# The first five levels of a DeltaNet chunk inverse on 32x32 diagonal squares of the TensorE array

## The chip, the cores and the metric

The kernel runs on one core of one Trainium2 chip, as one program. What is measured is device time in microseconds (us) of that core; the profile adds one traced execution with the start and end of every instruction on every engine. Of the engines, PE is the matrix unit (TensorE), PEld its loading of stationary operands (weights), DVE, ACT and POOL the vector, scalar and GpSimd engines, SP the queue that issues most DMAs.

## The reference

Two layers of a backbone. In each, 768 tokens (256 context, 512 latent) are projected, go through differential attention, grouped-query attention and a bidirectional gated DeltaNet side by side, are merged, and go through a channel mixer. The change is in the DeltaNet:

```python
a_low = jnp.where(strict, jnp.einsum('bhncd,bhnsd->bhncs', kb, kc) * decay, 0.0)
tmat = lax.linalg.triangular_solve(a_low + eye, jnp.broadcast_to(eye, a_low.shape),
                                   left_side=True, lower=True, unit_diagonal=True)
u = tmat @ (vc * bc[..., None])
w = tmat @ (kb * jnp.exp(gcum)[..., None])
```

For every chunk of tokens, head and direction, the inverse of a unit triangular matrix I + A is wanted. The kernel uses chunks of 128 tokens, so that a matrix fills a 128x128 square.

## The kernel before

The work on PE is of two kinds. The *lane* is long products: projections of all tokens with weights that are streamed from memory, written as runs of matmuls of 512 or 256 columns (their PSUM tiles are called `pf`, their weights `wl`). *Chains* are short dependent pieces: attention heads, norms, and the DeltaNet; their PSUM tiles are `pm` (one bank) and `pb`. A planner (`Sched`, with the estimate `Est` of when each engine gets through its queue) decides, as the program is built, which piece is queued next: a chain's piece when its inputs are estimated to be ready within 0.1 us, otherwise the next matmul of the lane. Every engine then works off its own queue strictly in that order. All recorded operations have one line, L166, that of the helper that records them, so groups are told apart by their tiles.

`dn_prep` is the chain that the change touches. It is run once for each of six steps of two pairs of heads in two layers, 24 times in all, each time for four units (two directions, two heads) that lie side by side in tiles of 512 columns. `a32` is I + A in float32, `a16` its float16 copy; both lie in workspace slots named `pres`. `u16` and `t16` (the inverse's transpose and the inverse, slots named `dnw`) start as the inverse of the diagonal and are doubled seven times, from blocks of 1 to blocks of 64:

- level 0: four matmuls of 128 columns with the identity transpose `a16` into a bank `py`; DVE masks it with `lev` into `u16`, and masks `a16` into `t16` in two more instructions;
- levels 1 to 6: four matmuls `a16` by `u16` of 128 columns into `py`; DVE multiplies the bank by the level's mask `lev` into `ym` (a `pres` tile); then four matmuls of 128 columns into `pt` and four of 64 columns into `pu`; ACT copies `pt` to `t16`, DVE the new columns from `pu` to `u16`;
- two Newton steps in higher precision follow, and then the scan over the chunks (`dn_pair`).

So each level puts two groups of matmuls on PE, with a DVE piece between them and an ACT and a DVE piece behind them, and in these pauses the planner queues the lane or another chain. Elsewhere in the program, `mod_mm` (the modulation, tiles `wm` and `wr` by `cond`) already divides the array by columns: its matmuls have 32 output rows each, at four places in turn.

Of the kernel before, what the change touches and what calls it, by code (L numbers as in the profile page):

```python
# [14 lines left out]
BF16 = mybir.dt.bfloat16  # L15
# [23 lines left out]
NLEV = 7  # L39
BIG = 1e30  # L40
# [33 lines left out]
class Est:  # L74
    """An estimate of when each engine gets through what is queued to it; it decides only the order in which
    independent pieces of work are queued."""
# [8 lines left out]
    def keys(self, ap):  # L85
        """The banks of a PSUM tile; the parts of a tile that was cut into views."""
# [12 lines left out]
    def cost(self, e, op, out, ins):  # L99
        n = out.free_size()  # L100
        if e == "P":
            cyc = (2 if op == "transpose" else 4) if ins[-1].dtype == F32 else 1
            return (max(n, 64) / 2.4 + 4) * (1 if out.shape[0] == 32 else cyc)
# [32 lines left out]
    def take(self, tag, t):  # L136
        """A tile of PSUM takes the place of the one that was given back first."""
        q = self.idle[tag]
        at = min(q)
        q.remove(at)  # L140
        for i in range(4 * t.tensor.shape[1] // 2048):
            self.done[t.tensor.name, i] = {"": at}, {}
        return t

    def give(self, tag, t):
        """A tile that nothing queued from here on touches."""
# [3 lines left out]
    def free(self, tag, n):  # L150
        """When the next n tiles of the tag can be had."""
        return sorted(self.idle[tag])[n - 1]
# [21 lines left out]
class Sched:  # L174
    """Queues chains of short dependent pieces as they become ready, and in between pieces of long products
    (the lane), of which one at a time is under way.

    A chain is a generator; it yields what its next piece needs: PSUM tags ("m", "mm", "b", ...), a time in ns
    to wait, or a condition (a function of true, or of the time from which it holds). A product is (units, body): units, the weights' sources; body(tiles) a generator."""
# [14 lines left out]
    def defer(self, gen, bank=None):  # L194
        """Work off the tensor engine, to be queued when the engines come to it; gen yields the engine of its next
        instruction, or a condition that an earlier group fulfils. It is the last to read bank."""
# [13 lines left out]
    def at(self, g):  # L210
        """When the next instruction of a group could start."""
# [4 lines left out]
    def settle(self):  # L216
        """Queues of the deferred work what would start soon."""
# [15 lines left out]
    def prefetch(self):  # L233
        """The first job's weights."""
# [3 lines left out]
    def flush_banks(self, n):  # L238
        """Leaves at most n banks of the lane to be read."""
# [4 lines left out]
    def stream(self, items, width, prio=0):  # L244
        """Chains (condition, generator, first need) in order, `width` of them at a time."""
        self.streams.append([list(items), width, prio, []])

    def room(self, need):
        """Whether the tiles are there: "w" slots of the workspace, "V" and "W" with one and with `reserve` to spare,
        "t" temporaries, "r" raw weights; "m", "b" PSUM."""  # L250
# [35 lines left out]
    def pick_fill(self, more):  # L286
        """A job that only fills gaps, of which there are so many and `more` to use."""
# [90 lines left out]
def trunk(  # L378
# [4 lines left out]
    rope, ident_d, tri_d, sel_d, m12_d, lev_d,  # L383
# [21 lines left out]
    def open_pools(nb, nm):  # L405
        """PSUM besides the feature projections' banks: nb pairs of banks and nm banks, until close_pools."""
# [12 lines left out]
    def whole(parts, n, nm, dt=F32):  # L419
        """One 6 KB slot of the workspace, in parts of n columns."""  # L420
# [9 lines left out]
    def q_tiles():  # L430
        """Per query chunk: four transposed columns of 128."""
        return slot(3, 512, "qt", F32R) + slot(3, 512, "qt", F32R)

    def drop(n=1):
        """n slots that nothing queued from here on touches."""
# [18 lines left out]
    def give(*banks):  # L454
        """Banks of psml that nothing queued from here on touches."""
# [22 lines left out]
    lev = const.tile([P, NLEV, 2, P], BF16, name="lev")  # L478
    nc.gpsimd.dma_start(out=lev, in_=lev_d)
    ones = const.tile([P, 1], F32, name="ones")  # L480
# [4 lines left out]
    def rsqrt_small(dst, src):  # L485
        """dst = src ** -0.5 on GpSimd; both [128, n] in SBUF."""
        G.tensor_tensor(out=dst, in0=src, in1=mhalf[:, 0:src.shape[1]], op=ALU.pow)

# [1 line left out]
    lo_n = [0, 3]  # L490

    def wunit(src, n):
        """A unit of weights, hi and lo, and the group that splits it."""
# [20 lines left out]
    def split(hi, lo, src, eng=None):  # L514
        """hi + lo == src, each with what a float32r matmul keeps."""
# [26 lines left out]
    def mod_mm(ps, raw, q, i, first, last):  # L542
        """256 columns of the modulation, of both streams at once, from half q of k: partitions 32 j + 2 i and the next
        sum over k = j and j + 4 (mod 8), the others get zeros; mod_sum adds them up and turns them to feature-major."""
# [4 lines left out]
    def mod_sum(m, b, sb, c0, n):  # L549
        """n pairs of column chunks from c0 on."""  # L550
# [9 lines left out]
    def mod_gen(m, b, cb, raws):  # L560
        """Four column chunks of the modulation."""
# [9 lines left out]
    def mod_late(l, m, b, pairs, room, pace):  # L571
        """A chain: up to MOD_N pairs of column chunks, the raw weights in slots of the workspace or in those of the products'."""
# [53 lines left out]
    def norm_acc(x, nt, out=None, fin=None, sq1=None):  # L626
        """Sums of squares over the chunks of x, as they come: add(chunk, first token, last) is a group; stats(first
        token, last) then gives the rows of (mean(x * x) + eps) ** -0.5 on all partitions of a bank. fin(first token,
        last, condition) is called when the last chunk has come; stats may be called once the condition holds."""
# [1443 lines left out]
```

## Time and profile before

| | |
|---|---|
| time, median of 3 runs | 2926.34 us (2926.0 to 2927.13) |
| span of the profiled execution | 2919.9 us |
| PE busy | 2847.6 us, 98% |
| PEld busy | 2466.7 us, 84% |
| DVE busy | 1693.0 us, 58% |
| ACT busy | 1226.7 us, 42% |
| POOL busy | 801.8 us, 27% |
| mean granted TensorE clock | 0.995 |

The busy time of an engine is the union of its instructions. For PE that is no measure of how fast it goes, since a matmul is listed from its start to the modelled end of its results, while the next one starts earlier; the distance from start to start is what a matmul costs its successors. The DeltaNet's preparations lie in two stretches, from about 575 to 930 us (layer one) and from 2140 to 2430 us (layer two).

### The profile page before, as it was taken

How to read it: one execution, taken by the hardware profiler on the slowest of the kernel's cores; microseconds unless marked ns; L12 is line 12 of the kernel's file. 1: busy time of each engine (PE TensorE's matmuls, PEld its weight loads, DVE VectorE, ACT ScalarE, POOL GpSimd, SP SyncE). 2: the span in 40 equal slices, each digit the busy share in tenths (PEclk: the TensorE clock that was granted, in tenths of full speed). 3: DMA queues.
4: the chain of work that ended last, by engine and by line, in shares of the span. 5: the costliest groups of instructions: out<-in, count | busy, mean ns of one | idle time of the engine just before them, and what ended most of it. 6: DMA issues, size and time to landing. Idle time of an engine off the chain costs nothing. (4 is left out here: it accounts for less than half of the span.)

```text
span 2919.9 us, 48983 instructions
## 1 busy us (share of the span) xinstructions
PE 2847.6 (98%) x19399; PEld 2466.7 (84%) x19399; DVE 1693.0 (58%) x3432; ACT 1226.7 (42%) x2522; POOL 801.8 (27%) x832
## 2 busy tenths in 40 slices
PE   7999999999999999999999999999999999999999
PEld 5888898888888888888888888998888787888888
DVE  4555667867766544334333456567788777553343
ACT  4444656644444223213222345466655443343332
POOL 3314231022322332102121233432133323422221
PEclk9999999999999999999999999999999999999999
DMA  8242211142112632342212222121111125323332
GB/s 300 95 146 82 68 47 56 48 157 66 65 57 84 242 105 93 113 124 68 73 49 75 76 97 66 36 78 55 61 41 45 55 72 185 130 87 104 97 99 87
DMA packets 96596, 268.82 MB, mean 92 GB/s; under 512 B 13808, under 2 KB 22896, under 8 KB 96368
## 3 DMA queue, kind: packets, MB, share of 16 engines
q1 hardware_dynamic: 85280, 244.13, 25.7%
q10 hardware_dynamic: 10800, 20.98, 1.8%
q8 instruction: 153, 2.51, 0.4%
q0 software_dynamic: 288, 0.59, 0.1%
q14 instruction: 75, 0.61, 0.1%
HBM read 237.41 MB, written 28.84 MB: 91 GB/s over the span
## 5 line engine op out<-in xcount | busy, mean ns | idle before, releaser
L166 PE MATMUL pf<-hh,wl 128*128 128x512 f32 (+1 forms) x4192 | 1020.8, 359 | 9.4 <-ACT hh L166 6.1
L166 PEld LDWEIGHTS pf<-hh,wl 128*128 128x128 f32 x4192 | 696.4, 189 | 106.6 <-issue 10.1
L166 POOL TENSOR_TENSOR wl<-wr,wl 128x512 fp32r<-128x512 f32 (+3 forms) x258 | 322.4, 1266 | 970.7 <-ACT wl L166 966.6
L166 PE MATMUL pf<-hl,wl 128*128 128x512 f32 (+1 forms) x2096 | 580.0, 359 | 0.9 <-POOL hl L166 0.5
L166 ACT CAST wl<-wr 128x512 fp32r<-128x512 f32 (+3 forms) x620 | 340.8, 589 | 491.8 <-PE pf L166 366.3
L166 PEld LDWEIGHTS pf<-hl,wl 128*128 128x128 f32 x2096 | 360.4, 189 | 47.5 <-issue 2.5
L166 PE MATMUL pf<-wl,hh 128*128 128x256 f32 (+2 forms) x1664 | 322.2, 288 | 0.0
L166 PE MATMUL pf<-g,wl 128*128 128x512 f32 (+1 forms) x1629 | 309.2, 350 | 0.0
L166 DVE TENSOR_TENSOR wl<-wr,wl 128x512 fp32r<-128x512 f32 (+4 forms) x362 | 260.9, 745 | 76.3 <-ACT wl L166 74.7
L166 PEld LDWEIGHTS pf<-g,wl 128*128 128x128 f32 x1629 | 263.4, 189 | 44.9 <-issue 2.9
L166 PEld LDWEIGHTS pf<-wl,hh 128*128 128x128 f32 x1664 | 265.0, 193 | 6.0 <-issue 4.1
L166 PE MATMUL pf<-wl,hl 128*128 128x256 f32 (+2 forms) x832 | 241.3, 290 | 0.0
L166 DVE SCALAR_TENSOR_TENSOR x<-pf,gate,x 128x512 f32<-128x512 f32 (+1 forms) x126 | 80.3, 639 | 230.5 <-PE pf L166 230.4
L166 PE MATMUL pm<-dnw,pres 128*128 128x128 f16 (+1 forms) x1824 | 197.2, 236 | 6.7 <-DVE dnw L166 2.1
L166 ACT ACTIVATE p<-pb,nb,r 128x768 f32<-128x768 f32 (+1 forms) x160 | 145.1, 908 | 104.8 <-DVE nb L166 82.9
L166 DVE SCALAR_TENSOR_TENSOR ff<-pf,cf,ff 128x511 f32<-128x511 f32 (+1 forms) x132 | 86.8, 658 | 172.9 <-ACT ff L166 171.5
L166 PE MATMUL pf<-ohl,wl 128*128 128x512 f32 (+1 forms) x864 | 168.2, 355 | 0.4 <-DVE th L166 0.4
L166 PEld LDWEIGHTS pf<-wl,hl 128*128 128x128 f32 x832 | 160.3, 193 | 2.7 <-issue 2.5
L166 PEld LDWEIGHTS pf<-ohl,wl 128*128 128x128 f32 x864 | 142.2, 189 | 23.4 <-DVE th L166 0.8
L166 DVE TENSOR_REDUCE mx<-pb 128x1 f32<-128x768 f32 (+1 forms) x160 | 133.5, 845 | 43.0 <-PE pb L166 41.8
L166 POOL TENSOR_TENSOR g<-ff,g 128x768 fp32r<-128x768 f32 (+1 forms) x44 | 69.8, 1586 | 256.8 <-ACT g L166 256.8
L166 ACT CAST dnw<-pm 128x512 f16<-128x512 f32 x144 | 83.8, 585 | 129.9 <-PE pm L166 124.5
(243 smaller groups left out, 4123.1 us busy)
## 6 DMA issues: line engine op xcount, KB each, us to landing
wr<-in_w_dram SPq DMA_DIRECT2D x88, 512.0 KB, 3.5
wr<-in_w_f_dram SPq DMA_DIRECT2D x80, 512.0 KB, 3.6
wm<-in_w_mod_dram SPq DMA_DIRECT2D x72, 512.0 KB, 6.2
wr<-in_w_t_dram SPq DMA_DIRECT2D x32, 512.0 KB, 3.6
wr<-in_w_br_dram SPq DMA_DIRECT2D x24, 512.0 KB, 3.6
wr<-in_w_mod_dram SPq DMA_DIRECT2D x24, 512.0 KB, 3.5
wr<-in_w_dram SPq DMA_DIRECT2D x32, 384.0 KB, 3.1
wr<-in_w_dram SPq DMA_DIRECT2D x32, 320.0 KB, 2.9
```

The costliest lines, as they stand in the source:

```text
L166: ins = f(*args, **kw)
```

## The change

Levels 0 to 4 fill blocks of at most 32, so they act within the four 32x32 squares on the diagonal of each unit. The changed kernel takes these squares out of `a32` (four ACT copies of 32 partitions and 4 x 32 columns, one for each square's partitions, into `ac`), and does levels 0 to 4 on tiles of 128 partitions and 4 x 32 columns, in which the partitions 32q to 32q + 31 hold square q of each unit. A matmul of such a level takes its weights and its moving operand from partitions 32q on and writes to partitions 32q on, so it uses one of four 32x32 places on the diagonal of the array; the helper `squares` issues 16 of them, unit by unit, the four places in turn. Level 0 is one such group of 16; levels 1 to 4 are a group of 16 and one of 32 each. The masks (`sub`) and copies then handle 128 columns instead of 512, and the copy of both results is one ACT instruction of 256 columns. At the end of level 4 two DVE instructions of 512 columns spread the squares over the full tiles `u16` and `t16`, with zeros elsewhere (`own`). Levels 5 and 6 and the Newton steps are as before, with a shorter `lev`. The planner prices a 32x32 matmul of up to 32 columns at 9 ns. Comments and docstrings were removed, which shifts lines: L166 is L170 in the changed kernel.

```diff
@@ class Est: cost
         if e == "P":
+            if out.shape[0] == SUB and n <= SUB:
+                return 9
             cyc = (2 if op == "transpose" else 4) if ins[-1].dtype == F32 else 1
@@ constants
-    lev = const.tile([P, NLEV, 2, P], BF16, name="lev")
+    lev = const.tile([P, NLEV - NSUB, 2, P], BF16, name="lev")
     nc.gpsimd.dma_start(out=lev, in_=lev_d)
+    sub = const.tile([P, NSUB + 1, 2, SUB], BF16, name="sub")
+    nc.gpsimd.dma_start(out=sub, in_=sub_d)
+    own = const.tile([P, P // SUB, SUB], BF16, name="own")
+    nc.gpsimd.dma_start(out=own, in_=own_d)
@@ dn_prep
+        for q in range(0, P, SUB):
+            S.copy(out=ym[q:q + SUB, 0:P].rearrange("p (u c) -> p u c", u=4), in_=a3[q:q + SUB, :, q:q + SUB])
         S.copy(out=a16, in_=a32)
...
+        def squares(out, a, b):
+            for u in range(4):
+                for q in range(0, P, SUB):
+                    r = slice(q, q + SUB)
+                    T.matmul(out[r, u * SUB:(u + 1) * SUB], lhsT=a(r, u), rhs=b(r, u), start=True, stop=True)
...
+        def masked(out, src, m):
+            V.tensor_tensor(out=d4(out), in0=d4(src), in1=sub[:, m].unsqueeze(2).to_broadcast([P, 2, 2, SUB]), op=ALU.mult)
+        ac, yc, tc_, uc_ = [ym[:, i * P:(i + 1) * P] for i in range(4)]
         py = psml()
-        for sl, *_ in un:
-            T.matmul(py[:, sl], lhsT=a16[:, sl], rhs=ident16, start=True, stop=True)
-        V.tensor_tensor(out=v4(u16), in0=v4(py), in1=lev[:, 0].unsqueeze(2).to_broadcast([P, 2, 2, P]), op=ALU.mult)
+        squares(py, part(ac), lambda r, u: ident16[r, r])
+        masked(uc_, py[:, 0:P], 0)
         give(py)
-        for d in range(2):
-            V.tensor_tensor(out=v4(t16)[:, d], in0=v4(a16)[:, d], in1=lev[:, 0, 1 - d].unsqueeze(1).to_broadcast([P, 2, P]), op=ALU.mult)
+        masked(tc_, ac, NSUB)
...
-        for lv in range(1, NLEV):
+        for lv in range(1, NSUB):
+            py = psml()
+            squares(py, part(ac), part(uc_))
+            masked(yc, py[:, 0:P], lv)
+            give(py)
+            yield "m"
+            pt = psml()
+            squares(pt, part(yc), part(tc_))
+            squares(pt[:, P:2 * P], part(tc_), part(yc))
+            if lv < NSUB - 1:
+                S.copy(out=ym[:, 2 * P:4 * P], in_=pt[:, 0:2 * P])
+            else:
+                for full, src in ((u16, pt[:, P:2 * P]), (t16, pt[:, 0:P])):
+                    V.tensor_tensor(out=full.rearrange("p (u q c) -> p u q c", u=4, q=P // SUB),
+                                    in0=src.rearrange("p (u c) -> p u c", u=4).unsqueeze(2).to_broadcast([P, 4, P // SUB, SUB]),
+                                    in1=own.unsqueeze(1).to_broadcast([P, 4, P // SUB, SUB]), op=ALU.mult)
+            give(pt)
+            yield "m"
+        for lv in range(NSUB, NLEV):
             b = 1 << lv
...
-            V.tensor_tensor(out=v4(ym), in0=v4(py), in1=lev[:, lv].unsqueeze(2).to_broadcast([P, 2, 2, P]), op=ALU.mult)
+            V.tensor_tensor(out=v4(ym), in0=v4(py), in1=lev[:, lv - NSUB].unsqueeze(2).to_broadcast([P, 2, 2, P]), op=ALU.mult)
```

On PE, at the first levels of the first preparation of layer one: before, a level's first group (`pm<-dnw,pres`, four matmuls of 128 columns) and its second one (four more and four of 64 columns, `pm<-pres,dnw`) stand among matmuls of the lane (`pf`); here the second group of one chain follows on the first of another.

```order
L166 MATMUL pf<-hl,wl 128x256 x2
L166 MATMUL pf<-hh,wl 128x256 x3
L166 LDWEIGHTS pres
L166 MATMUL pm<-dnw,pres 128x128
...
L166 LDWEIGHTS dnw
L166 MATMUL pm<-pres,dnw 128x64
...
L166 MATMUL pf<-hh,wl 128x256
L166 MATMUL pf<-hl,wl 128x256
```

And the same engine now, at levels 1 and 2 of the same preparation:

```order
L170 MATMUL pf<-hl,wl 128x512 x2
L170 MATMUL pf<-hh,wl 128x512
L170 LDWEIGHTS pres
L170 MATMUL pm<-pres 32x32
...
L170 MATMUL pf<-hh,wl 128x512 x3
L170 MATMUL pf<-hl,wl 128x512 x2
L170 LDWEIGHTS pres
L170 MATMUL pm<-pres 32x32
...
L170 MATMUL pb<-identr,p 128x128 x4
L170 MATMUL pf<-hh,wl 128x512
```

The groups still alternate with matmuls that use the whole array. Over the whole program the matmuls of 32x32 are 4992, in 211 unbroken runs (103 of them of 16 and 90 of 32 matmuls).

On ACT, at the start of the first preparation, before (`pres<-pres` is the copy of I + A to float16):

```order
L166 ACTIVATE p,sums_6960<-pb,nb,r_4946 128x768
L166 ACTIVATE pres<-pres,ngc 128x128 x3
L166 CAST pres<-pres 128x512
L166 ACTIVATE pres<-pres,ngc 128x128
L166 CAST wl<-wr 128x512
L166 COPY otmp<-pm 64x256
```

and now:

```order
L170 ACTIVATE p,sums_6964<-pb,nb,r_4950 128x768
L170 ACTIVATE pres<-pres,ngc 128x128 x3
L170 CAST pres<-pres 32x128 x4
L170 CAST pres<-pres 128x512
L170 COPY otmp<-pm 64x256
L170 ACTIVATE pres<-pres,ngc 128x128
```

The four copies of squares stand ahead of the copy of the whole, and the first group of small matmuls waits for them.

## Rows read from the trace of the kernel before

**Rows 1.** The page's first part: busy us of each engine, instructions.
```profile
PE 2847.6 (98%) x19399; PEld 2466.7 (84%) x19399; DVE 1693.0 (58%) x3432; ACT 1226.7 (42%) x2522; POOL 801.8 (27%) x832
```

**Rows 2.** Stretches of 60 us: busy us (and instructions) of PE, PEld, DVE, ACT, POOL; clock; DMA.
```profile
600.00:660.00 60.00, 59.96 (x587) 49.52 (x586) 41.72 (x91) 24.73 (x57) 14.70 (x16) 1.00 0.48 166
2160.00:2220.00 60.00, 57.07 (x501) 47.61 (x500) 50.07 (x99) 32.16 (x72) 24.33 (x26) 1.00 0.12 36
2580.00:2640.00 60.00, 60.00 (x265) 49.33 (x264) 23.58 (x37) 19.28 (x36) 15.87 (x13) 1.00 0.31 92
```

**Rows 3.** PE's waits over the whole span: for whom, total us, times, longest.
```profile
PE pm L166 <- DVE pres L166: 6.9, 6, 2.1
PE pm L166 <- DVE dnw L166: 2.8, 4, 1.3
PE pm L166 <- POOL pres L166: 1.9, 4, 0.6
```

**Rows 4.** Timeline of PE, DeltaNet stretch: start us, us to the modelled end, operation, count.
```profile
661.58 0.40 PE L166 MATMUL pm<-dnw,pres 128*128 128x128 f16 x4
661.79 0.71 PE L166 MATMUL pf<-hh,wl 128*128 128x512 f32 x2
662.34 0.40 PE L166 MATMUL pm<-dnw,pres 128*128 128x128 f16 x4
662.57 0.28 PE L166 MATMUL pm<-pres,dnw 128*128 128x64 f16 x4
662.69 0.94 PE L166 MATMUL pf<-hh,wl 128*128 128x512 f32 x3
663.47 0.40 PE L166 MATMUL pm<-dnw,pres 128*128 128x128 f16 x4
```

**Rows 5.** The same, at 16 matmuls that divide the array by columns.
```profile
666.63 1.07 PE L166 MATMUL pm<-wm,cond 128*32 128x256 f32 x16
667.64 0.40 PE L166 MATMUL pm<-dnw,pres 128*128 128x128 f16 x4
```

**Rows 6.** Timeline of PE at eight such matmuls between lane matmuls.
```profile
1231.29 0.39 PE L166 MATMUL pf<-hh,wl 128*128 128x512 f32 x1
1231.61 0.64 PE L166 MATMUL pm<-wr,cond 128*32 128x256 f32 x8
1232.18 0.96 PE L166 MATMUL pf<-hh,wl 128*128 128x512 f32 x3
1232.98 0.40 PE L166 MATMUL pf<-hl,wl 128*128 128x512 f32 x1
```

**Rows 7.** The weight loads (PEld) of those eight, from the same timeline.
```profile
1231.61 0.16 PEld L166 LDWEIGHTS pm<-wr,cond 128*32 128x32 f32 x8 [0.35 <-issue]
```

**Rows 8.** The weight loads by shape, 1231 to 1233.2 us: count, busy us, mean ns, idle.
```profile
L166 PEld LDWEIGHTS pm<-wr,cond 128*32 128x32 f32 x8 | 0.2, 108 | 0.4 <-issue 0.4
```

**Rows 9.** Instructions on the tiles pres and dnw: count, ns min/median/max, first to last.
```profile
L166 DVE TENSOR_TENSOR pres<-pm,lev x144: 672/684/693, 598.6 to 2420.3; 128x512 f16<-128x512 f32 x144
L166 DVE TENSOR_TENSOR dnw<-pres,lev x48: 277/283/1380, 584.4 to 2396.9; 128x256 f16<-128x256 f16 x48
L166 ACT CAST pres<-pres x24: 603/619/622, 583.8 to 2394.7; 128x512 f16<-128x512 f32 x24
...
L166 ACT CAST dnw<-pm x144: 563/586/603, 606.3 to 2422.0; 128x512 f16<-128x512 f32 x144
L166 DVE CAST dnw<-pm x144: 406/424/426, 606.3 to 2422.3; 128x256 f16<-128x256 f32 x144
L166 ACT ACTIVATE dnw<-dnw,gc x96: 384/392/414, 577.0 to 2390.9; 128x128 f32<-128x128 f32 x96
```

**Rows 10.** Groups by shape, 600 to 960 us: count, busy us, mean ns, idle before.
```profile
L166 DVE TENSOR_TENSOR oacc<-pm,oacc 128x128 f32<-128x128 f32 x24 | 5.8, 281 | 3.6 <-PE pm L166 3.6
L166 ACT ACTIVATE th<-pf 128x256 f32<-128x256 f32 x10 | 3.9, 386 | 7.1 <-PE pf L166 7.1
```

More of the change, by code (lines that the diff above doesn't have):

```diff
@@ L39 @@
 NLEV = 7
+NSUB = 5
+SUB = 32
 BIG = 1e30
@@ L382, in trunk @@
     qk_g, lam_in, sub_g, conv_dn, a_log, dt_b, dn_g, conv_ff, bias_ff,
-    rope, ident_d, tri_d, sel_d, m12_d, lev_d,
+    rope, ident_d, tri_d, sel_d, m12_d, lev_d, sub_d, own_d,
     out, dbg=None,
@@ L1457, in dn_prep, with part, d4 @@
         yield "m"
+        def squares(out, a, b):
[3 more added lines that the diff above has]
+                    T.matmul(out[r, u * SUB:(u + 1) * SUB], lhsT=a(r, u), rhs=b(r, u), start=True, stop=True)
+        def part(t):
+            return lambda r, u: t[r, u * SUB:(u + 1) * SUB]
+        def d4(t):
+            return t.rearrange("p (d i c) -> p d i c", d=2, i=2)
+        def masked(out, src, m):
+            V.tensor_tensor(out=d4(out), in0=d4(src), in1=sub[:, m].unsqueeze(2).to_broadcast([P, 2, 2, SUB]), op=ALU.mult)
+        ac, yc, tc_, uc_ = [ym[:, i * P:(i + 1) * P] for i in range(4)]
         py = psml()
-        for sl, *_ in un:
-            T.matmul(py[:, sl], lhsT=a16[:, sl], rhs=ident16, start=True, stop=True)
-        V.tensor_tensor(out=v4(u16), in0=v4(py), in1=lev[:, 0].unsqueeze(2).to_broadcast([P, 2, 2, P]), op=ALU.mult)
+        squares(py, part(ac), lambda r, u: ident16[r, r])
+        masked(uc_, py[:, 0:P], 0)
         give(py)
-        for d in range(2):
-            V.tensor_tensor(out=v4(t16)[:, d], in0=v4(a16)[:, d], in1=lev[:, 0, 1 - d].unsqueeze(1).to_broadcast([P, 2, P]), op=ALU.mult)
+        masked(tc_, ac, NSUB)
         if any(t < nq for _, _, _, t, _ in un):
@@ L2009, in _consts @@
     sel = np.tile(np.eye(32), (4, 1))
-    return [np.ascontiguousarray(a, np.float32) for a in (rope, np.eye(P), tri, sel, m12, lev)]
+    own = np.zeros((P, P // SUB, SUB), np.float32)
+    own[i, i // SUB] = 1.0
+    sq = np.stack([lev[q:q + SUB, :NSUB, :, q:q + SUB] for q in range(0, P, SUB)]).reshape(P, NSUB, 2, SUB)
+    sub = np.concatenate([sq, sq[:, 0:1, ::-1]], 1)
+    return [np.ascontiguousarray(a, np.float32) for a in (rope, np.eye(P), tri, sel, m12, lev[:, NSUB:], sub, own)]
 def prepare(x, c, ctx, c_ctx, w_mod, b_mod, norm1_g, w_in, da_qn_g, da_kn_g, da_lambda, da_subln_g,
@@ L2052 @@
 _NAMES = ['xT', 'condT', 'w_mod', 'b_mod', 'n_g', 'w_t', 'w_kv', 'w_f', 'w_br', 'w_o', 'w_1', 'w_2', 'qk_g', 'lam', 'sub_g',
-          'conv_dn', 'a_log', 'dt_b', 'dn_g', 'conv_ff', 'bias_ff', 'rope', 'ident', 'tri', 'sel', 'm12', 'lev']
+          'conv_dn', 'a_log', 'dt_b', 'dn_g', 'conv_ff', 'bias_ff', 'rope', 'ident', 'tri', 'sel', 'm12', 'lev', 'sub', 'own']
 def kernel(**inputs):
```

## The prediction

> **What bounds the kernel now.** I read the page's first part, the table of 60 us stretches, PE's waits, and then timelines of PE. PE is busy 98% of the span [rows 1], and in the DeltaNet stretches it is hardly less (59.96 and 57.07 us of 60, at the full clock of 2.4 GHz, granted 1.00 [rows 2]), while DVE has 42 to 50 us there and ACT 25 to 32. PE's waits that the preparations' tiles end, those on `pres` and `dnw`, come to 6.9 + 2.8 + 1.9 = 11.6 us in the whole program [rows 3]. So time is set by what PE's queue costs from start to start, and a chain that is shorter in itself can give back at most those 11.6 us. Busy time says nothing about that cost, so I price PE's pieces by starts. A lane matmul of 512 columns costs 60 / 265 = 0.226 us in a stretch that holds little else [rows 2].
>
> **A group of the chain, before.** The first group of a level (four matmuls of 128 columns) starts at 661.58 and the lane at 661.79: 0.21 us. The two lane matmuls behind it take 0.55 us to the next group, 0.10 more than 2 x 0.226: the price of going into and out of a chain's group, in which a lane matmul waits for its longer weight load. Together 0.31 us. The second group runs from 662.34 to 662.69, 0.35 us, and the three lane matmuls behind it take 0.78 us instead of 0.68, again 0.10: 0.45 us. So a level costs PE 0.76 us and level 0, one group of four, 0.31 us [rows 4].
>
> **A group of small matmuls, after.** It has two parts, the matmuls and the change of the array's division.
>
> The matmuls: no 32x32 matmul stands in the trace. From below: eight weight loads at four column places lie within 0.16 us, of which the last one's own is 0.108, so seven steps take 0.05, some 7 ns each [rows 7, 8]: a matmul and its load can be issued every 7 ns when the places differ. From above: matmuls of 64 columns on the whole array, 0.12 us for four [rows 4], are 30 ns each; that would be the price if the four places did not overlap at all. A place comes round every fourth matmul, and at 30 ns a round the four make 7 to 8 ns each. I take 7: the rows with a divided array are the nearest, and a round agrees with them. A group of 16 is then 0.11 us and one of 32 is 0.22.
>
> The division: a lane matmul ahead of a group by columns is followed after 0.32 us instead of 0.226 [rows 6]: 0.09 to get in. Eight such matmuls take 0.57 us to the next start [rows 6], sixteen 1.01 [rows 5], so eight more cost 0.44, and 0.13 of the 0.57 is not theirs: the way out. The three lane matmuls behind take 0.80 instead of 0.68 [rows 6], 0.12 more. Sum 0.34 us a group, against 0.10 for a chain's group that leaves the array whole. In a plain sequence a matmul starts some 0.16 us before the modelled end of the one ahead (662.34 against 661.79 + 0.71 [rows 4]); at a change of division only 0.07 before (667.64 against 666.63 + 1.07 [rows 5]). The array is being emptied, both ways. A place of 32 rows may empty sooner than one of 128, which no row shows; so the bounds are 0.10 (no price for the change) and 0.34, and I take 0.30, near the row that has a change in it.
>
> A group of 16 is then 0.41 us, one of 32 is 0.52. A level costs 0.93 to 0.94 instead of 0.76, +0.176 us, 24 x 4 = 96 times: **+16.9 us**. Level 0 costs 0.41 instead of 0.31, 24 times: **+2.4 us**. The order lists 211 runs of small matmuls instead of 24 x 9 = 216, five changes fewer: **-1.5 us**. All of this lies on PE's queue, where nothing hides it. The matmuls alone are a saving, 4992 x 7 ns = 35 us in place of 24 x (0.21 + 4 x 0.56) = 59 us; what eats it is 211 times 0.20 us of emptying.
>
> **The other engines.** A preparation loses on DVE five masks of 0.684, two of 0.283 and four copies of 0.424 [rows 9], 5.7 us. It gains five masks of 128 columns, some 0.281 each [rows 10], one from SBUF (at most 0.283) and two spreads of 512 columns, 0.684 each by the mask's row: 3.1 us. ACT loses four copies of 0.586 [rows 9] and gains three of 256 columns, 0.386 by the nearest row [rows 10], and four of 128 columns, 0.392 [rows 9]: +0.4 us. Over 24 preparations DVE has 63 us less and ACT 9 us more; neither is the bound, so neither sum counts by itself. Two more loads of masks are issued by POOL at the start, while PE waits for its inputs, and cost nothing there.
>
> The chain itself: levels 1 to 3 lose 0.40 on the mask and 0.20 on the copy, and gain the 0.18 that PE costs more, -0.42 us each. Level 0 has 0.69 less on DVE and 0.10 more on PE, -0.59. Level 4 has 0.40 less on the mask, 0.18 more on PE, and ends in two DVE instructions in a row, 1.37 us, instead of a copy of 0.59: +0.56. And the first group waits for four ACT copies (1.57 us) where it waited for one of 0.62: +0.95. Sum -0.3 us for a preparation: the chain gets hardly shorter. What is left is DVE's queue, 10% emptier in these stretches. Of the 11.6 us of waits [rows 3] I take off 4, with bounds of 0 and 11.6: **-4 us**. The planner prices a group at 9 ns a matmul (0.14 and 0.29 us), so PE comes to later pieces later than planned, which also makes their inputs earlier, not later.
>
> **The sum.** 16.9 + 2.4 - 1.5 - 4 = +13.8 us. The profiled execution has a span of 2919.9 us and the median is 6.4 us above it, which stays: 2926.3 + 13.8 = **2940 us**, 0.5% slower. Its own range is 2933 to 2952 (0.34 us a group gives +8.6 more, all waits gone 7.6 less).
>
> **Rivals.** *The change of division is nearly free (faster).* Were a small group as cheap to enter and leave as a chain's group is now, 0.10 us, a level would cost 0.54 instead of 0.76: -21.5 us, level 0 -2.4, the waits -4: **2898 us**. The place is the border between a group and the lane. It decides below 0.24 us a group, where the sum is zero; from 0.21 to 0.26 the two kernels are within 0.2%. For it: no row shows 32x32 places, and they have a quarter of the rows to empty. Against it: each border in [rows 5, 6] shows the same 0.09 us, with lane matmuls of other widths and weights.
>
> *The four places do not run side by side (much slower).* At 30 ns each, 4992 x 23 ns = 115 us more: **3055 us**; at half that, 15 ns, **2980 us**. It decides from the first row of 32x32 starts. For it: the trace shows places by columns only, none by rows and columns. Against it: 7 ns from place to place in [rows 7].
>
> Beside this rival stands a rule of the Trainium skill ("TensorE: Matmul & The Clock Gate", Part 1, on the gap of 56 ns): the distance between the starts of two matmuls never falls below about 25 ns, however few columns they have. By it the sum would have 4992 x 18 ns, 90 us, more and come to 3030 us; the trace agrees for matmuls on the whole array, 30 ns [rows 4], and not for different places, 7 ns [rows 7].
>
> *The waits go altogether and more (level).* The lane's matmuls are fixed, so an emptier DVE can give no more than [rows 3]: 2926.3 + 17.8 - 11.6 = 2932.5, still at the edge of slower; with 0.26 us a group, 2924. *The change does nothing to the order:* excluded, the order shows the small groups between lane matmuls.
>
> **How the numbers follow.** A run of this kernel can tell 0.2%, 5.9 us, from no change. Forecast (0.26 to 0.34 us a group, 7 to 9 ns a matmul): 0.50, of which 0.06 falls under 2932 by the waits. Cheaper change of division, under 0.26: 0.33, of which 0.24 ends below 2920 and 0.09 near the old time. Places that overlap only in part: 0.11; not at all: 0.06. So faster 0.24, same 0.15, slower 0.61. The range leaves out the cheapest changes of division (0.10) and places that hardly overlap (0.10): 2906 to 2982, which takes in half an overlap.
>
> **What would show it.** In the profile after: small matmuls some 7 ns apart within a group, each place coming round in about 30 ns; a start only 0.07 us before the modelled end of the last at both borders of a group; 0.41 and 0.52 us from group to lane, extra waits of the next lane matmul included. PE's waits on `pres` and `dnw` under 11.6 us in all; DVE's busy time near 1630 us, ACT's near 1236. The DeltaNet stretches should hold the whole difference, half in each layer. I am wrong if starts at the borders come as close as 0.16 us before the end, or if a group of 32 takes much over 0.3 us from first to last start.

## The result, and the profile after

The changed kernel takes 2949.9 us (median of 4 runs, 2947.1 to 2951.8), the kernel before 2926.2 us in the runs beside it: ratio 1.0082, 95% interval 1.0070 to 1.0094, 0.8% slower. The profiled execution spans 2947.9 us against 2919.9, 28.0 us more. About 16 us of that arise in layer one's DeltaNet and 12 in layer two's; the rest of the program is level in sum. Executions of one kernel differ, and the profiled one of the kernel before is a quick one: the spans differ by 28.0 us and the medians by 23.7, so what is read below from single executions holds to about 5 us.

The page's first part of the changed kernel (busy us, share, instructions), to be read against [rows 1]:

```profile
PE 2867.0 (97%) x23143; PEld 2464.7 (84%) x23143; DVE 1633.8 (55%) x3360; ACT 1225.6 (42%) x2594; POOL 801.5 (27%) x834
```

PE has 3744 matmuls more and is busy 19.4 us longer. DVE has 59.2 us less, ACT 1.1 less. Span less PE's busy time gives its idle time: 72.3 us before, 80.9 now.

PE's waits of the changed kernel over the whole span (for whom, total us, times, longest), against [rows 3]:

```profile
PE pm L170 <- DVE pres L170: 9.1, 10, 2.7
PE pm L170 <- DVE dnw L170: 4.6, 6, 1.0
PE pm L170 <- POOL pres L170: 1.9, 4, 1.3
PE pm L170 <- issue: 1.2, 2, 0.8
```

The three rows that were 11.6 us are 15.6, with the preparations' new ACT copies (1.1 us) 16.7. They were to shrink.

Two of the stretches of 60 us of the changed kernel (busy us and instructions of PE, PEld, DVE, ACT, POOL; granted clock; DMA share, GB/s), against [rows 2]:

```profile
600.00:660.00 60.00, 59.60 (x1039) 46.52 (x1037) 36.53 (x88) 24.87 (x64) 13.21 (x15) 1.00 0.43 156
2160.00:2220.00 60.00, 57.95 (x948) 46.95 (x946) 41.48 (x92) 30.95 (x76) 18.97 (x22) 1.00 0.11 34
```

PE is as full as before, and DVE has 36.5 and 41.5 us instead of 41.7 and 50.1: the relief that the prediction counted on is there.

PE's timeline in the changed kernel, two places where small groups stand between lane matmuls of 256 columns (start us, us to the modelled end, operation, count), against [rows 4]:

```profile
850.41 0.40 PE L170 MATMUL pf<-hh,wl 128*128 128x256 f32 x2
850.74 0.27 PE L170 MATMUL pm<-pres 32*32 32x32 f16 x16
850.94 0.50 PE L170 MATMUL pf<-hh,wl 128*128 128x256 f32 x2
851.28 0.40 PE L170 MATMUL pf<-hl,wl 128*128 128x256 f32 x2
...
853.77 0.37 PE L170 MATMUL pm<-pres 32*32 32x32 f16 x32
854.07 0.74 PE L170 MATMUL pf<-hh,wl 128*128 128x256 f32 x4
854.65 0.40 PE L170 MATMUL pf<-hl,wl 128*128 128x256 f32 x2
```

Sixteen matmuls take 0.20 us to the next start and thirty-two 0.30: sixteen more cost 0.10 us, **6.4 ns each** by the unrounded starts (99 and 199 ns from first to last). The rest is the border. Behind a group, four lane matmuls take 0.58 us (854.07) and two 0.34 (850.94), so two cost 0.24 and the first one waits 0.10 more. The first small start comes 0.33 us after two lane matmuls (850.41), 0.09 more than their 0.24, and the next lane start 0.10 us after the last small one. The medians over all groups of 16 and 32 are 0.09 to 0.10 in, 0.10 out and 0.10 to 0.11 on the next lane matmul: **0.30 us a group beside the matmuls**. Both borders show the sign that the prediction named: the next start 0.07 us before the modelled end (850.41 + 0.40 against 850.74; 850.74 + 0.27 against 850.94).

The other engines' new pieces, against [rows 9, 10]. DVE's instructions on the two tiles in the changed kernel (count, ns min/median/max, first to last):

```profile
L170 DVE TENSOR_TENSOR pres<-pm,sub x120: 274/284/293, 589.2 to 2440.9; 128x128 f16<-128x128 f32 x120
L170 DVE TENSOR_TENSOR pres<-pres,sub x24: 213/222/1328, 582.7 to 2424.5; 128x128 f16<-128x128 f16 x24
...
L170 DVE TENSOR_TENSOR dnw<-pm,own x48: 680/683/692, 605.5 to 2443.7; 128x512 f16<-128x512 f32 x48
```

ACT's groups by shape, 600 to 960 us (count, busy us, mean ns, idle before):

```profile
L170 ACT CAST pres<-pm 128x256 f16<-128x256 f32 x34 | 12.6, 372 | 44.4 <-PE pm L170 39.3 <-DVE dnw L170 4.9
L170 ACT CAST pres<-pres 32x128 f16<-32x128 f32 x40 | 11.7, 294 | 13.8 <-DVE pres L170 13.1
```

**Where a long wait comes from.** PE's timeline of the changed kernel at 715 us (in brackets the idle time before an instruction and what ended it):

```profile
715.53 0.37 PE L170 MATMUL pm<-pres 32*32 32x32 f16 x32 [1.96 <-DVE pres L170]
```

DVE's timeline of the same time:

```profile
714.85 0.42 DVE L170 TENSOR_TENSOR kv<-pm,rkd 128x256 f32<-128x256 f32 x1 [2.71 <-POOL rkd L170]
715.19 0.28 DVE L170 TENSOR_TENSOR pres<-pm,sub 128x128 f16<-128x128 f32 x1
```

And POOL's:

```profile
711.45 1.27 POOL L170 TENSOR_TENSOR wl<-wr,wl 128x512 fp32r<-128x512 f32 x1 [13.12 <-ACT wl L170]
712.69 0.23 POOL L170 TENSOR_SCALAR rkd<-rkd 128x2 f32<-128x2 f32 x1
712.88 1.26 POOL L170 TENSOR_TENSOR wl<-wr,wl 128x512 fp32r<-128x512 f32 x1
714.11 0.71 POOL L170 TENSOR_TENSOR rkd<-rkd,mhalf 128x2 f32<-128x2 f32 x1
```

PE stands 1.96 us for a mask of 0.28 us. The mask stands in DVE's queue behind `kv<-pm,rkd`, which needs the reciprocal root of 128x2 numbers from POOL, and POOL has put a weight split of 1.26 us between the two small steps of that root. The wait of 2.65 us at 790 us is of the same kind with another root: DVE sits idle 2.69 us for POOL's `fb`, and then its instruction of 128x6 on `fb` takes 1.22 us beside POOL's next split, where the median of that instruction is 0.17. Behind both waits the clock falls. The first place in two stretches (us; busy us and instructions of PE, PEld, DVE, ACT, POOL; granted clock; DMA share, GB/s):

```profile
710.00:716.40 6.40, 4.39 (x116) 3.27 (x115) 3.40 (x11) 2.58 (x6) 3.37 (x4) 1.00 0.17 55
716.40:719.80 3.40, 3.40 (x40) 1.85 (x39) 2.36 (x7) 0.96 (x2) 0.00 (x0) 0.51 0.14 55
```

PE was busy 4.39 of 6.4 us, and the next 3.4 us are granted the lower level, 1.2 GHz. The whole span has 41.0 us at that level, before 30.7. Four stretches of 3.4 us, from 668.6, 716.4, 791.4 and 951.9 us, are in or just behind layer one's DeltaNet, at or behind waits of 1.0 to 2.7 us; the kernel before has none there, although PE waits 2.06 us at 750.5 us in it.

**The account** used from here on: span = PE idle + half of the time at the lower level (what it costs if PE is busy in it) + the rest, which is *PE's queue* at full clock. Before: 72.3 + 15.4 + 2832.3. After: 80.9 + 20.5 + 2846.5. So of the 28.0 us, **14.2 are PE's queue, 8.6 waits, 5.1 clock**, to the 5 us that single executions allow.

### The profile page after: what moved, and what is told of

It reads as the page before. It is cut to its first block, busy times and chain, and to the rows that moved or that the text cites. A ratio compares the mean times of both kernels' runs of the same rounds, so it can differ in the third digit from the quotient of the medians.

```text
span 2947.9 us, 56407 instructions
## 1 busy us (share of the span) xinstructions
PE 2867.0 (97%) x23143; PEld 2464.7 (84%) x23143; DVE 1633.8 (55%) x3360; ACT 1225.6 (42%) x2594; POOL 801.5 (27%) x834
## 5 line engine op out<-in xcount | busy, mean ns | idle before, releaser
L170 PE MATMUL pf<-hh,wl 128*128 128x512 f32 (+1 forms) x4192 | 1020.8, 360 | 11.3 <-ACT hh L170 8.1
L170 PEld LDWEIGHTS pf<-hh,wl 128*128 128x128 f32 x4192 | 696.9, 190 | 113.2 <-ACT hh L170 10.7
L170 POOL TENSOR_TENSOR wl<-wr,wl 128x512 fp32r<-128x512 f32 (+3 forms) x258 | 323.1, 1270 | 988.6 <-ACT wl L170 920.4
L170 PE MATMUL pf<-hl,wl 128*128 128x512 f32 (+1 forms) x2096 | 576.0, 360 | 1.4 <-POOL hl L170 1.1
L170 ACT CAST wl<-wr 128x512 fp32r<-128x512 f32 (+3 forms) x620 | 340.6, 588 | 500.8 <-PE pf L170 379.8
L170 PEld LDWEIGHTS pf<-hl,wl 128*128 128x128 f32 x2096 | 361.4, 190 | 51.8 <-issue 2.9
L170 PE MATMUL pf<-wl,hh 128*128 128x256 f32 (+2 forms) x1664 | 321.9, 288 | 0.0
L170 PE MATMUL pf<-g,wl 128*128 128x512 f32 (+1 forms) x1629 | 309.2, 350 | 0.6 <-ACT g L170 0.6
L170 DVE TENSOR_TENSOR wl<-wr,wl 128x512 fp32r<-128x512 f32 (+4 forms) x362 | 259.0, 741 | 82.9 <-ACT wl L170 81.3
L170 PEld LDWEIGHTS pf<-g,wl 128*128 128x128 f32 x1629 | 263.4, 189 | 45.5 <-ACT g L170 2.9
L170 PEld LDWEIGHTS pf<-wl,hh 128*128 128x128 f32 x1664 | 264.9, 193 | 6.0 <-issue 4.1
L170 PE MATMUL pf<-wl,hl 128*128 128x256 f32 (+2 forms) x832 | 241.1, 290 | 0.0
L170 DVE SCALAR_TENSOR_TENSOR x<-pf,gate,x 128x512 f32<-128x512 f32 (+1 forms) x126 | 80.4, 640 | 230.1 <-PE pf L170 225.6
L170 ACT ACTIVATE p<-pb,nb,r 128x768 f32<-128x768 f32 (+1 forms) x160 | 145.1, 908 | 104.9 <-DVE nb L170 84.4
L170 DVE SCALAR_TENSOR_TENSOR ff<-pf,cf,ff 128x511 f32<-128x511 f32 (+1 forms) x132 | 86.9, 659 | 172.5 <-ACT ff L170 171.1
L170 PE MATMUL pf<-ohl,wl 128*128 128x512 f32 (+1 forms) x864 | 168.4, 355 | 0.9 <-DVE th L170 0.5
L170 PEld LDWEIGHTS pf<-wl,hl 128*128 128x128 f32 x832 | 160.1, 192 | 2.7 <-issue 2.5
L170 PEld LDWEIGHTS pf<-ohl,wl 128*128 128x128 f32 x864 | 142.0, 189 | 24.2 <-DVE th L170 0.9
L170 DVE TENSOR_REDUCE mx<-pb 128x1 f32<-128x768 f32 (+1 forms) x160 | 133.6, 846 | 41.5 <-PE pb L170 40.4
L170 PEld LDWEIGHTS <-pres 32*32 32x32 f16 (+1 forms) x5568 | 81.4, 90 | 76.5 <-issue 36.5
L170 POOL TENSOR_TENSOR g<-ff,g 128x768 fp32r<-128x768 f32 (+1 forms) x44 | 69.7, 1584 | 256.5 <-ACT g L170 256.5
L170 PE MATMUL pm<-dnw,pres 128*128 128x128 f16 (+1 forms) x1056 | 124.5, 247 | 4.5 <-DVE dnw L170 2.4
```

The lines of the kernel that those rows point to most:

```text
L170: ins = f(*args, **kw)
```

## Experiments

All times are medians; each ratio is to runs of the kernel before on the same chip (whose median there is 2925.3 to 2926.8). "Changes" counts runs of small matmuls on PE; the last four columns are of the profiled execution, in us.

| kernel | median us | ratio [95%] | changes | span | PE idle | at half clock | PE's queue |
|---|---|---|---|---|---|---|---|
| before | 2926.2 | 1 | 0 | 2919.9 | 72.3 | 30.7 | 2832.3 |
| after | 2949.9 | 1.0082 [1.0070, 1.0094] | 211 | 2947.9 | 80.9 | 41.0 | 2846.5 |
| e1_whole | 2893.5 | 0.9891 [0.9877, 0.9906] | 0 | 2890.4 | 71.1 | 27.3 | 2805.6 |
| e2_price | 2959.9 | 1.0120 [1.0103, 1.0137] | 204 | 2957.0 | 81.1 | 68.3 | 2841.7 |
| e3_split | 2962.2 | 1.0126 [1.0111, 1.0141] | 308 | 2960.4 | 70.0 | 41.0 | 2870.0 |
| e4_twice | 3027.6 | 1.0351 [1.0335, 1.0367] | 189 | 3022.5 | 103.0 | 105.8 | 2866.7 |
| e5_dear | 2964.3 | 1.0127 [1.0111, 1.0144] | 182 | 2967.8 | 87.6 | 88.7 | 2835.9 |
| e6_after_lag | 2941.9 | 1.0052 [1.0037, 1.0067] | 195 | 2946.5 | 69.1 | 75.1 | 2839.9 |
| e7_before_lag | 2931.4 | 1.0019 [1.0010, 1.0029] | 0 | 2931.9 | 77.4 | 37.5 | 2835.7 |
| e8_pairs | 2937.9 | 1.0042 [1.0029, 1.0054] | 115 | 2933.1 | 79.5 | 54.6 | 2826.3 |
| v1_bd | 2930.8 | 1.0016 [1.0006, 1.0025] | 0 | 2930.2 | 86.0 | 51.2 | 2818.7 |
| v2_bd_lag | 2925.3 | 0.9996 [0.9987, 1.0005] | 0 | 2922.8 | 79.9 | 51.2 | 2817.3 |
| v3_pairs_lag | 2967.4 | 1.0138 [1.0123, 1.0154] | 111 | 2965.3 | 96.5 | 92.2 | 2822.8 |

**Theory:** what PE's queue gained is the price of changing the array's division. **Rival:** it is the small matmuls themselves, or the chain's latency.

### Does the division cost it?

Each sixteen small matmuls become four on the whole array (e1_whole). The other instructions stay; their order shifts a little, since the planner prices four such matmuls at 123 ns and sixteen small ones at 144:

```diff
-    for q in range(0, P, SUB):
-        r = slice(q, q + SUB)
-        T.matmul(out[r, u * SUB:(u + 1) * SUB], lhsT=a(r, u), rhs=b(r, u), start=True, stop=True)
+    T.matmul(out[:, u * SUB:(u + 1) * SUB], lhsT=ident16, rhs=m(u), start=True, stop=True)
```

> The changed kernel, with each 16 small matmuls replaced by four matmuls of 32 columns on the whole array (identity as weights, so the inverse is not computed; the tiles, masks, copies, waits and the rest are those of the changed kernel). Theory (the array is emptied at both borders of each of 211 runs of small matmuls, about 0.2 us a run): without any change of division a group of 16 becomes some 0.12 us and one of 32 some 0.23, plus 0.10 for going in and out, so a level costs PE 0.55 instead of 0.90 us and level 0 0.22 instead of 0.40: 34 + 4 = 38 us less than the changed kernel, 2908 to 2914 us, below the kernel before. Rival (the division costs nothing, the loss comes from the chain on the other engines and the waits it makes): 2940 to 2950 us, no better than the changed kernel.

It is 56.4 us under the changed kernel, even beyond the theory, and falls on its side. PE's queue is 40.9 us shorter, as forecast; 9.8 us of idle time and 6.9 of clock came on top. A group of four takes 0.11 us to the next start here (median), and sixteen small ones take 0.10 from first to last, so the matmuls themselves are not what costs; the division is. The next lane matmul still loses 0.09 us behind a group, so of the 0.30 us about 0.20 are the division's.

A further change of division inside each group of 32 (e3_split):

```diff
 squares(pt, part(yc), part(tc_))
+T.matmul(pt[:, 2 * P:2 * P + 64], lhsT=ident16, rhs=ident16[:, 0:64], start=True, stop=True)
 squares(pt[:, P:2 * P], part(tc_), part(yc))
```

> The changed kernel with one more matmul on the whole array (64 columns, into an unused part of the bank) in the middle of each of the 96 groups of 32 small matmuls, so that each group changes the division twice more. Theory: each of the 96 costs some 0.03 us for itself and 0.20 us for emptying the array twice, 19 to 25 us more than the changed kernel, 2969 to 2975 us. Rival (a change of division costs nothing): 96 x 0.03 = 3 us more, 2950 to 2954 us.

The time rose by 12.3 us, between the two. The account tells why: PE's queue rose by 23.5 us, 96 times 0.24, as forecast, and idle time fell by 10.9. PE's timeline of this kernel at one such group:

```profile
664.94 0.27 PE L170 MATMUL pm<-pres 32*32 32x32 f16 x16
665.15 0.20 PE L170 MATMUL pm<-ident 128*128 128x64 f16 x1
665.28 0.27 PE L170 MATMUL pm<-pres 32*32 32x32 f16 x16
665.48 0.97 PE L170 MATMUL pf<-hl,wl 128*128 128x512 f32 x3
```

From first small start to lane it is 0.54 us instead of 0.30. One whole-array matmul of 64 columns in the middle costs 0.24, of which 0.03 are its own.

### The price of a matmul, and a limit that no theory had

Each group of 16 is issued twice (e4_twice):

```diff
-for u in range(4):
+for u in (0, 1, 2, 3, 0, 1, 2, 3):
```

> The changed kernel with every group of 16 small matmuls issued twice in a row (the second time over the same output), so 4992 more small matmuls and not one change of division more. Theory (the four places run side by side at 6.5 ns a matmul): 32 us more than the changed kernel, 2978 to 2985 us. Rival (starts in the trace are not what they cost, a small matmul costs 25 to 30 ns): 125 to 150 us more, 3075 us and above.

Both are wrong: +78 us lies between the two forecasts, for a reason neither gave. The first 32 starts of a run are still 6.4 ns apart on average (199 ns). From the 33rd on they are 8.3 ns apart (16 in 133 ns): a run of 64 takes 473 ns and one of 96 takes 762, where 6.4 ns would make 403 and 608. And some runs stop in the middle for 0.5 to 2.9 us: 2 of the 85 runs of 32 matmuls, 8 of the 82 of 64 and 8 of the 15 longer ones. From first to last start all runs take 99.7 us, in the changed kernel 34.3; of the 65 us more, 21 are such idle time. PE's timeline of e4_twice at two pauses:

```profile
814.82 0.34 PE L170 MATMUL pm<-pres 32*32 32x32 f16 x26
816.76 0.73 PE L170 MATMUL pm<-pres 32*32 32x32 f16 x70 [1.60 <-issue]
817.42 0.62 PE L170 MATMUL pf<-hl,wl 128*128 128x256 f32 x3
817.88 0.95 PE L170 MATMUL pm<-identr,oacc 128*128 128x128 f32 x4
818.76 0.58 PE L170 MATMUL pm<-pres 32*32 32x32 f16 x51
820.23 0.54 PE L170 MATMUL pm<-pres 32*32 32x32 f16 x45 [0.89 <-issue]
```

The DMA queues from 814 to 817 us (queue, kind: packets, MB, share of the 16 engines), one line in all:

```profile
q8 instruction: 1, 0.02, 2.0%
```

And the first pause itself as a stretch (columns as above):

```profile
815.16:816.76 1.60, 0.00 (x0) 0.00 (x0) 0.00 (x0) 0.00 (x0) 0.00 (x0) 1.00 0.00 0
```

For 1.6 us no engine does anything, and the releaser is "issue": nothing that the profile shows. The only DMA packet from 814 to 817 us is one of the queue of kind "instruction", and it starts at 814.56. PE resumes 2.20 us behind that start. The other pauses of this kind lie the same way: packet at 817.83 and resumption at 820.23, 821.29 and 823.70. Over the whole program that queue moves, in the kernel before:

```profile
q8 instruction: 153, 2.51, 0.4%
```

In the changed kernel:

```profile
q8 instruction: 182, 2.98, 0.4%
```

And in e4_twice:

```profile
q8 instruction: 221, 3.62, 0.5%
```

The step from the second to the third is 0.64 MB for 2 x 4992 instructions, 64 bytes each; a packet (16 KB) is then 256 instructions, 128 matmuls with their loads. From the one resumption to the next PE starts 70 + 3 + 4 + 51 = 128 matmuls, just one packet, and up to the third, at 823.70, 128 again. PE eats a packet in 0.8 to 1.1 us at 6.4 to 8.3 ns. So long runs of small matmuls drain the instruction supply, and waits on "issue" total 27.4 us here (1.2 in the changed kernel); no run changed the supply itself. PE often idles at the lower clock here, so the account's split between queue and clock isn't exact for this kernel.

### Is it the planner's price?

The planner takes 9 ns a matmul and nothing for a change. Given the real price (e2_price), and a price far too high (e5_dear):

```diff
-                return 9
+                return 6.5      # e2_price; there also: start += 100 at each change of division
+                return 30       # e5_dear
```

> The changed kernel, computing the same, with only the planner's price altered: 6.5 ns for a small matmul and 0.1 us for every change of division, near what the trace shows, in place of 9 ns and nothing. Theory (PE is later than the planner thinks, so work of POOL and DVE that hangs on the lane comes later than planned and DVE's queue stands behind it; PE's waits on pres and dnw are 4 to 6 us more than before, and the clock falls to half after three of them): the waits go back, 5 to 12 us less than the changed kernel, 2938 to 2945 us, but not below the kernel before. Rival (the waits are chance, or the price decides more than the array does): no change, or 2926 us and less.

> The changed kernel with the planner's price of a small matmul at 30 ns instead of 9 (a group of 16 at 0.48 and of 32 at 0.96 us, above the 0.40 and 0.50 that the trace shows with both borders). PE's queue costs the same; only the order changes. If PE's waits and the falls of the clock follow from a wrong price, a price from above brings them down and the time moves 5 to 15 us towards the kernel before, 2935 to 2945 us. If they are a matter of how the pieces happen to fall, the time stays within 10 us of the changed kernel on either side, 2940 to 2960 us.

Both came out slower, by 10 and 14 us, outside every forecast. PE's queue is shorter (-4.8 and -10.6 us, with 7 and 29 changes fewer), idle time is level or longer (+0.2, +6.7), and the time at the lower clock rises from 41 to 68 and 89 us. The waits on the preparations' tiles are 13.4 and 16.8 us instead of 16.7. A stretch of e5_dear in which nearly only small matmuls run (columns as above):

```profile
842.20:849.00 6.80, 6.09 (x236) 4.48 (x235) 2.79 (x10) 2.75 (x7) 2.51 (x2) 1.00 0.28 95
849.00:859.20 10.20, 8.59 (x183) 5.82 (x183) 5.13 (x10) 1.33 (x3) 0.00 (x0) 0.50 0.08 31
```

PE is busy 6.09 of 6.8 us ahead of the fall, 213 of its 236 matmuls on the preparations' tiles, and then has 10.2 us at half clock. Why the clock falls here is not shown. Neither price took the waits away: with nearly the right one they are still above the 11.6 us of the kernel before.

### Does DVE's queue behind POOL make the long waits?

DVE's instruction that needs POOL's root is queued later, in the changed kernel (e6_after_lag), the kernel before (e7_before_lag) and the variant of the next section (v2_bd_lag):

```diff
 rsqrt_small(r2, r)
-yield
+yield max(0.0, est.end - est.t["P"]) + 3000
```

> The changed kernel, but the DVE instruction that needs the small reciprocal root from POOL (in the heads' norms and in the DeltaNet's finish) is put into DVE's queue about 3 us later by the planner's clock, so that other DVE work can stand ahead of it. Theory (the long waits of PE end at a DVE tile whose queue stood behind that POOL result, 2.6 and 2.7 us in the two places read): waits on pres and dnw fall from 16.7 us to about 10, the half-clock time behind them by some 3 us, so 2940 to 2945 us. Rival (the waits are how the pieces happen to fall, and any new order deals new ones): no systematic change, 2945 to 2960.

> The same edit of the order in the kernel before. Theory: it has one such wait (2.06 us at 750.5), so 2923 to 2926 us, 0 to 3 us less. Rival (waits are how the pieces fall): anything from 2920 to 2940, with waits on pres and dnw that are as long but elsewhere.

PE's waits of e6_after_lag:

```profile
PE pm L170 <- DVE pres L170: 3.8, 7, 1.6
...
PE pm L170 <- issue: 2.9, 4, 1.0
PE pm L170 <- POOL pres L170: 2.4, 4, 1.0
```

In the changed kernel it does what the theory says: the waits on the preparations' tiles fall from 16.7 to 7.5 us and the time by 8.0. The clock did not follow (75.1 us at half clock in the profiled execution, which was the slowest of its four). In the kernel before it fails: 6 us slower, waits 13.2 instead of 11.6. So the chain POOL to DVE to PE is real where it is seen, but taking it away deals a new order with waits of its own, and the rival holds as a general statement.

### The same inverse without a changed division

The squares are spread by DVE to block-diagonal weights of 128x128, and each product is four matmuls of 32 columns on the whole array, with a spread of 0.42 us on DVE for each new weight (v1_bd):

```diff
-squares(py, part(ac), part(uc_))
+squares(py, u16, part(uc_))
...
+def spread(full, src):
+    V.tensor_tensor(out=full.rearrange("p (u q c) -> p u q c", u=4, q=P // SUB),
+                    in0=src.rearrange("p (u c) -> p u c", u=4).unsqueeze(2).to_broadcast([P, 4, P // SUB, SUB]),
+                    in1=own.unsqueeze(1).to_broadcast([P, 4, P // SUB, SUB]), op=ALU.mult)
```

> A version that computes the same inverse without dividing the array: the moving operands of levels 0 to 3 are the narrow tiles of 4 x 32 columns, as in the changed kernel, but the weights are full 128x128 tiles that are zero outside the squares, spread from the narrow tiles by DVE (two spreads of 512 columns in SBUF a level); level 4 writes full tiles. A level is 4 + 8 matmuls of 32 columns. Theory (the change of division is what costs): PE per level 0.55 us instead of 0.76 in the kernel before at levels 1 to 3, 0.76 at level 4, 0.22 instead of 0.31 at level 0: 0.72 us a preparation, 17 us in all below the kernel before; DVE has some 37 us more work than before, which may bring waits of 0 to 10 us: 2908 to 2920 us. Rival (any narrowing of the chain's pieces upsets the order and costs waits): no better than the kernel before, 2926 us and above.

> The same edit in the variant without a changed division, which has its 22.4 us of waits against the 11.6 of the kernel before and its longest one behind such a POOL result (5.8 us of DVE at 2240). Theory: the waits fall by 8 to 15 us and the clock gives back some 5: 2912 to 2922 us, under both kernels. Rival: no systematic change, 2925 to 2935.

PE's queue is 13.6 us under that of the kernel before, where 17 were forecast, and waits and clock take it all back: idle +13.7, half-clock time +20.5 (costing 10). The time, 2930.8, misses the forecast of 2908 to 2920 and lies where the rival had it. The longest wait, in PE's timeline of v1_bd:

```profile
2241.44 1.27 PE L168 MATMUL pm<-dnw,pres 128*128 128x128 f32 x5 [4.03 <-DVE dnw L168]
```

DVE's ahead of it:

```profile
2240.28 0.42 DVE L168 TENSOR_TENSOR kv<-pm,rkd 128x256 f32<-128x256 f32 x1 [5.78 <-POOL rkd L168]
```

And POOL's, the same two small steps, this time with a split ahead of them and four scalings ahead of that:

```profile
2235.67 2.34 POOL L168 TENSOR_SCALAR pres<-pres,beta 128x128 f32<-128x128 f32 x4
2237.97 1.26 POOL L168 TENSOR_TENSOR wl<-wr,wl 128x512 fp32r<-128x512 f32 x1
2239.20 0.23 POOL L168 TENSOR_SCALAR rkd<-rkd 128x2 f32<-128x2 f32 x1
2239.52 0.72 POOL L168 TENSOR_TENSOR rkd<-rkd,mhalf 128x2 f32<-128x2 f32 x1
```

With the later place (v2_bd_lag) the waits on the preparations' tiles fall from 22.4 to 16.2 us and the time to 2925.3: level with the kernel before, not under it, and again in the rival's range.

### Fewer changes, same matmuls

Two preparations of a pair of steps wait for each other ahead of each small group, so that their groups stand together (e8_pairs; with the later place, v3_pairs_lag):

```diff
+def both(k):
+    at = meet.setdefault((hp, s // 2, k), [])
+    at.append(max(est.end, est.t["P"]))
+    return lambda: len(at) == 2 and sch.room("m") and max(*at, est.free("m", 1))
...
-yield "m"
+yield both(2 * lv)
```

> The changed kernel with one thing added: two preparations that belong together (steps 0 and 1, 2 and 3, 4 and 5 of a pair of heads) wait for each other ahead of each group of small matmuls, so that their groups stand in PE's queue one behind the other. Same matmuls, same sizes; the order lists 115 runs of small matmuls instead of 211, most of 32 and 64. Theory (the cost is 0.30 us for each change of the array's division, whatever stands between two changes): 96 changes fewer, PE's queue 29 us shorter, so about 2921 us, with waits and half-clock time as they fall from 2915 to 2935. Rival (the cost lies in the matmuls or in the exposed weight loads of a group's members, which stay): within 5 us of the changed kernel, or over it.

> The same with the later place in DVE's queue for the instruction that needs POOL's small reciprocal root; 111 runs of small matmuls. Theory: PE's queue 30 us shorter than the changed kernel's and waits that end at DVE's pres and dnw below 10 us: 2910 to 2925 us, under both kernels. Rival (two chains that come together ask for DVE and the banks together, so waits grow by what the changes give back; and long stretches of mostly small matmuls bring more time at the half clock): 2925 to 2950.

e8_pairs is 12 us under the changed kernel, against 29 expected and a rival that allowed 5; its 2937.9 is just over the forecast's 2915 to 2935. PE's queue fell by 20.2: 96 changes at 0.30 are 28.8, and 7.5 came back inside the longer runs, whose later matmuls are slower as in e4_twice (a run of 64 takes 496 ns, two of 32 take 398). It also pauses for instructions, 5.6 us in all. Its two longest waits on "issue", in PE's timeline:

```profile
608.08 0.21 PE L170 MATMUL pm<-pres 32*32 32x32 f16 x6
610.11 0.62 PE L170 MATMUL pm<-pres 32*32 32x32 f16 x58 [1.81 <-issue]
...
613.67 0.35 PE L170 MATMUL pm<-pres 32*32 32x32 f16 x28
616.03 0.46 PE L170 MATMUL pm<-pres 32*32 32x32 f16 x36 [2.01 <-issue]
```

Instruction packets start at 607.82 and 613.71, 2.3 us ahead of either resumption. So the theory of the price holds for PE's queue, with these limits on how far grouping helps. v3_pairs_lag has a queue as short (2822.8) and is 17.5 us slower than the changed kernel: idle +15.6, half-clock time +51. The forecast of waits below 10 us was wrong (20.1), which is past even the rival.

## Why the prediction was right or wrong

The direction was right, and so was the main term, the price of changing the division; the term for the waits was not. The time, 2949.9, is 10 us over the 2940 named and just inside the forecast's own range of 2933 to 2952. That it is inside is luck in part: the upper end was made of 0.34 us a group and waits that stay as they are, and what filled that room were longer waits and time at the lower clock. The 6.4 us between the traced span and the median, which were to stay, are 2.0 after; they were in part the draw of one execution.

- **PE's queue.** The level, level 0 and run terms came to +17.8 us; measured +14.2. The price of a change, 0.34 by the matmuls that divide the array by columns [rows 5, 6] and taken as 0.30, is 0.30 for 32x32 places, and the starts at their borders come 0.07 us before the modelled end as there. The first rival fell with it. The 7 ns a matmul, the step of the column places' weight loads [rows 7, 8], were 6.4 between starts: 4992 x 0.6 ns is 3 of the 3.6 us that the term was too large, though single executions are not exact enough to say so.
- **Places side by side.** They are: sixteen matmuls at four places start within 0.10 us. The rival of 3055 us and its half fell. The Trainium skill ("TensorE: Matmul & The Clock Gate", Part 1, on the gap of 56 ns) gives a least distance of about 25 ns between starts. The measured 6.4 ns between different places speak against it here, and e4_twice shows the same 6.4 ns in runs of 32 and 8.3 behind them; one and the same place comes round every 26 ns.
- **The waits: the step that failed.** The sum took off 4 us, with bounds of 0 and 11.6 off; idle time rose by 8.6 us, of which the preparations' tiles have 5.1. Two assumptions were wrong. A less busy DVE was taken to shorten waits, but PE's two longest waits begin with DVE standing idle for POOL, 2.71 and 2.69 us, with the mask behind it in the queue. No run tested DVE's load by itself. And "PE comes to later pieces later than planned, which also makes their inputs earlier" does not hold: the inputs hang on an order of DVE's and POOL's queues that the change deals anew. Kernels with the very same matmuls and other orders (after, e2_price, e5_dear, e6_after_lag) lie from 2942 to 2964 us. A term for a dealt order needed bounds of about 10 us on both sides of zero.
- **The clock** was not in the sum. It cost +5.1 us by the two profiled executions; the stretches that are new stand at or behind waits of 1.0 to 2.7 us.
- **The other engines.** DVE forecast 1630, measured 1633.8; ACT forecast 1236, measured 1225.6, since a copy on 32 partitions takes 294 ns, not the 392 of [rows 9].

What stays open: why one order has 30 us at half clock and another 90. The falls stand behind waits and behind stretches of small matmuls, but no run separated the two, and the kernel before has a wait of 2.06 us with no fall behind it.

## What to carry to other kernels

Small matmuls at different places of the array are cheap; each going in and out of a division is not (0.30 us here, against 0.10 for a group that leaves the array whole). So a divided piece pays only where many of its matmuls stand together. Grouping helps only so far: from the 33rd matmul of a run on the starts were 8.3 ns apart instead of 6.4, and the longer the run, the more often it paused for instructions. Where a planner deals the order, forecast the bottleneck's queue by starts and give the waits and the clock a term with both signs; and read a long wait back through the in-order queues before crediting a less busy engine.

## What the runs showed of the hardware that was not expected

- Matmuls that go round four 32x32 places start 6.4 ns apart, so that each place has one every 26 ns; from the 33rd of a run on it is 8.3 ns.
- The instruction stream is itself a limit: packets of 16 KB (256 instructions), pauses in neighbouring packets just 128 matmuls apart, PE resuming 2.2 to 2.7 us behind the start of the packet it lacked, also with no other DMA under way.
- A DVE instruction with two inputs in SBUF can take three times as long beside POOL. DVE's timeline of v2_bd_lag:

```profile
2155.45 1.50 DVE L168 TENSOR_TENSOR pres<-cmp,own 128x512 f16<-128x512 f16 x1
```

  POOL's at the same time:

```profile
2155.20 1.47 POOL L168 TENSOR_TENSOR wl<-wr,wl 128x512 fp32r<-128x512 f32 x1
```

  The spread's median is 0.42 us, and here it ends 0.28 us after POOL's split. So do all 22 spreads of this kernel and all 28 of v1_bd that take over 0.6 us: each ends 0.28 us after a POOL instruction that began before it. The changed kernel's mask from SBUF has such a maximum too (1328 ns against a median of 222, above). The Trainium skill ("SBUF — State Buffer", the summary of rules for kernel authors) says that of a DVE instruction with two SBUF inputs and a GpSimd one that reads SBUF the later blocks until the first is done; these rows agree, and no run took the split away to show it.
